# Rotary embedding in a hybrid attention layer: the sine product and its sum on GpSimd instead of VectorE, rounding and low part half a step later

## Chip, cores and metric

One core of a Trainium2 chip runs the whole layer in one launch. The metric is the device time in microseconds (us) of one execution. Below, PE is TensorE (matmuls), PEld its weight loads, DVE is VectorE, ACT is ScalarE, POOL is GpSimd and SP is SyncE, which here only issues transfers.

## The reference

A decoder layer over 2048 positions and 1024 channels. The input is normalised and modulated, multiplied by one wide input matrix, and split for two mixers: a forgetting attention of 8 heads over all earlier keys, and a banded attention (window of 128) of 8 query heads and 2 key heads with rotary positions and one sink value per head. Both are gated, joined, projected, normalised and added to the residual. Cut to what matters here:

```python
h = rms_norm(x, g_pre[l]) * (1.0 + scale[:, None, :]) + shift[:, None, :]
proj = h @ w_in[l]
qa, ka, va, fa, za, qb, kb, vb, zb = jnp.split(proj, split_points, axis=-1)
oa = forgetting_attention(qa, ka, va, fa + b_fgate[l]) * jax.nn.silu(za)
qb, kb = rope(qb, positions), rope(kb, positions)
ob = sliding_window_sink_attention(qb, kb, vb, sinks[l]) * jax.nn.silu(zb)
y = jnp.concatenate([oa, ob], axis=-1) @ w_out[l]
x = x + gate[:, None, :] * rms_norm(y, g_post[l])

def rope(x, positions):
    ...
    x1, x2 = xf[..., :half], xf[..., half:]
    return jnp.concatenate([x1 * cos - x2 * sin, x2 * cos + x1 * sin], axis=-1)
```

## The kernel before

**Precision.** Every matmul operand is kept as two f16 numbers, a rounded high part and a low part (the rest), and a product is three matmuls: high by high, high by low, low by high. So each evacuation of a result has three steps: scale it, round it to f16 on ACT, and subtract on DVE to get the low part.

**Stages.** The kernel first computes the modulation and the transposed, normalised input hT for chunk 0 of four chunks of 512 positions. Then a long list of small units (`punits`) goes over PE: slices of the input projection, eight slices of three matmuls for a tile of 128 columns by one chunk. While the first chunks are projected, the input of the next chunks is normalised on DVE (L429, with the root computed on POOL, L108 to L122), transposed on PE (L435), scaled by ACT into hT's high part and a f32 copy hf (L441), and split by DVE (L445 rounds the odd slices, L446 subtracts). Then come 32 windows of the banded attention, woven between the rest of the projection slices, from some 150 to 394 us of the span. After that runs the forgetting attention, from some 400 us, and last the output projection.

**Order.** The order on each engine is written out by hand. `after(n, f)` puts a step on a list, and `tick()` runs what is due: a step put there with n runs at the n-th tick from then. In the prologue a tick comes after every two slices (`tick2`); in the windows there are four ticks a window. Within one tick the step that was put on the list earlier runs first. Every engine works its own instructions in this order, and an instruction that waits holds all that stand behind it on that engine. An issue of a transfer by POOL (`G.dma_start`) or SP stands in that engine's queue like any other instruction.

**The rotary evacuation** (`evac_rope`, L739 to L771) runs 20 times: for the keys (kb) of the four chunks, and for the queries (qb) of four tiles by four chunks. At tick 1 ACT copies the result to qf, and SP issues four copies of 32 partitions each that swap the halves of the heads into qs (L751). At tick 2 DVE multiplies the result by the cosine into qc (L754), which frees the PSUM bank. At tick 7 DVE multiplies qs by the sine (L764) and adds it to qc (L765). At tick 8 ACT rounds qc into stg (L768), and at tick 9 DVE subtracts for the low part (L758). For keys, `finish` then has SP store stg into kst (L779); for queries stg itself is what the scores read. There is one qs and one qf; qc comes from a pool of three tiles that the gates' evacuation (tz) uses too; stg comes from a pool of two for keys and of four for queries.

**A window** (`Pair`) has: scores on PE into one PSUM tile pss (L889); masking, maxima and their scaled negative b_nb on DVE (L897 to L904); four exponentials on ACT (L911); transposes on PE (L918); folding on ACT and DVE (L927, L928); four masking selects on POOL into ptb (L932, L934); the product with the values on PE (L946); scaling on DVE (L952), and the store of its parts by POOL (L292, L285). As pss is one tile, the scores of the next window wait for the exponentials of this one. A tile's weight column is prepared ahead: load (L221, POOL), maximum (L227, DVE), its way through DRAM to all partitions (L230 mx_d and L235 mxr, both issued by POOL, the second waiting for the first to land), scale (L246 to L253, DVE), high part (L267, ACT), low part (L273, DVE).

Of the kernel before, what the change touches and what calls it, by code (L numbers as in the profile page):

```python
# [15 lines left out]
AF = mybir.ActivationFunctionType  # L16
ALU = mybir.AluOpType
# [26 lines left out]
def hybrid_layer(  # L44
# [17 lines left out]
    V, A, G, PE, SP = nc.vector, nc.scalar, nc.gpsimd, nc.tensor, nc.sync  # L62
# [88 lines left out]
    sinT = swc.tile([P, S], F32, name="sinT")  # L151
# [50 lines left out]
    def after(n, f):  # L202
        late.append([n, f])
# [535 lines left out]
    def evac_rope(ci, finish, pool):  # L739
        cols_ = slice(ci * CH, (ci + 1) * CH)  # L740

        def evac(ps, free):
            qf = swt.tile([P, CH], F32, tag="qf", name="qf")
            qs = swt.tile([P, CH], F32, tag="qs", name="qs")
            qc = op_.tile([P, CH], F32, tag="tz", name="qc")
            stg = (pool or abp).tile([P, 2, CH], F16, tag="st", name="stb")

            def copy():
                A.activation(qf[:], ps, AF.Copy, scale=PS_SCALE)
                for r in range(4):  # L750
                    SP.dma_start(qs[32 * r:32 * r + 32, :], qf[32 * (r ^ 1):32 * (r ^ 1) + 32, :])  # L751

            def cos():
                V.scalar_tensor_tensor(qc[:], ps, PS_SCALE, cosT[:, cols_], op0=ALU.mult, op1=ALU.mult)  # L754
                free()

            def low():
                V.tensor_tensor(stg[:, 1, :], qc[:], stg[:, 0, :], op=ALU.subtract)  # L758
                finish(stg)

            after(1, copy)
            after(2, cos)
            def sine():
                V.tensor_tensor(qs[:], qs[:], sinT[:, cols_], op=ALU.mult)  # L764
                V.tensor_tensor(qc[:], qc[:], qs[:], op=ALU.add)  # L765

            after(7, sine)
            after(8, lambda: A.activation(stg[:, 0, :], qc[:], AF.Copy))  # L768
            after(9, low)

        return evac  # L771

# [1011 lines left out]
```

## Time and profile before

| what | value |
|---|---|
| median of 3 runs | 1157.98 us (1157.04 to 1157.98) |
| profiled execution, its own time | 1157.8 us |
| its span, first to last instruction | 1156.1 us |
| mean granted TensorE clock | 0.996 |
| sine product L764, 20 times on DVE, shortest / median / longest | 673 / 692 / 2251 ns |
| sum L765, 20 times on DVE | 691 / 692 / 2915 ns |
| rounding L768, 20 times on ACT | 629 / 630 / 641 ns |
| low part L758, 20 times on DVE | 678 / 692 / 1732 ns |

How its rows are read. The first part of the page gives each engine's busy time, share of the span and number of instructions. A row of groups names line, engine, operation, tiles (written <- read) and shapes, the count, then busy us and mean ns of one, then the engine's idle time just before it and what ended that. A row of the timeline starts with the start and the length in us, and ends in square brackets with the idle time before it and its releaser, where there was any. A row of waits names who waited for whom, with the total, the number of times and the longest. A row of one line's instructions has shortest, median and longest ns and the first and last start. A busy PE is no proof of matmuls at full rate, since they are pipelined and their ends are modelled.

### The profile page before, as it was taken

To read this page: it belongs to the slowest core of one execution; us is meant where nothing else is said; L and a number is where in the kernel's file an instruction comes from. 1 tells how busy PE (TensorE), PEld (TensorE's weight loads), DVE (VectorE), ACT (ScalarE), POOL (GpSimd) and SP (SyncE) were. 2 spreads that over 40 slices of the span, in tenths; PEclk is the share of its full clock that TensorE was granted. 3 is DMA by queue.
4 is the path that set the end of the run, shared out by engine and by line. 5 is a ranking of instruction groups with operands and counts; after the bars stand their busy time and mean duration, and the time that the engine had idled before them with its cause. 6 is when DMAs were issued, how large, how long until landed. Compare 5 with 4: busy or idle time off the path is not lost. (4 is left out here: it accounts for less than half of the span.)

```text
span 1156.1 us, 25291 instructions
## 1 busy us (share of the span) xinstructions
PE 1116.8 (97%) x9869; PEld 656.3 (57%) x9869; DVE 930.5 (80%) x2137; ACT 661.4 (57%) x1150; POOL 207.5 (18%) x332
## 2 busy tenths in 40 slices
PE   5899999999999999999999999999999999999997
PEld 2475544577765866555555555555555555544444
DVE  7877468987888568788988899888888887878885
ACT  2876344654555421666757666666776778534332
POOL 1122134554556530010010110001000000000000
PEclk9899999999999999999999999999999999999999
DMA  9943355433243232442344342123311337686743
GB/s 333 336 116 72 87 78 96 97 63 90 52 92 88 58 87 58 73 108 29 80 64 87 84 67 70 38 49 76 45 43 34 91 101 206 140 225 197 199 135 109
DMA packets 123476, 120.10 MB, mean 104 GB/s; under 512 B 64948, under 2 KB 100828, under 8 KB 123356
## 3 DMA queue, kind: packets, MB, share of 16 engines
q1 hardware_dynamic: 112088, 85.69, 27.6%
q0 software_dynamic: 10832, 32.50, 13.5%
q8 instruction: 77, 1.26, 0.6%
q14 instruction: 43, 0.35, 0.1%
q10 hardware_dynamic: 436, 0.28, 0.1%
HBM read 64.75 MB, written 25.18 MB: 78 GB/s over the span
## 5 line engine op out<-in xcount | busy, mean ns | idle before, releaser
L1356 ACT ACTIVATE p<-sta,lift,scl_qk 128x1024 f32<-128x1024 f32 (+2 forms) x160 | 172.0, 1075 | 131.6 <-PE sta L1350 82.6
L351 PE MATMUL bk<-hT,wh_qk 128*128 128x512 f16 x768 | 194.7, 378 | 0.0
L1363 DVE TENSOR_TENSOR pha<-p,pha 128x1024 f16<-128x1024 f32 (+2 forms) x160 | 169.1, 1057 | 0.2 <-ACT pha L1360 0.2
L1303 DVE TENSOR_REDUCE a_m<-bk 128x1 f32<-128x512 f32 x192 | 130.4, 686 | 45.8 <-PE bk L1300 44.8
L1576 PE MATMUL bk<-wohl,oz 128*128 128x512 f16 x744 | 165.3, 379 | 1.1 <-DVE oz L1525 0.7
L1360 ACT ACTIVATE pha<-p 128x1024 f16<-128x1024 f32 (+2 forms) x160 | 148.1, 926 | 5.9 <-PE poa L1376 1.2
L1576 PEld LDWEIGHTS <-oz 128*128 128x128 f16 x744 | 71.9, 99 | 82.8 <-DVE oz L1525 1.8
L1376 PE MATMUL poa<-vt,pha 128*128 128x65 f16 x1088 | 116.1, 192 | 1.4 <-DVE pha L1363 1.2
L1373 PE MATMUL poa<-vt,pha 128*128 128x65 f16 x1088 | 116.6, 193 | 0.8 <-DVE ona L1382 0.7
L1375 PE MATMUL poa<-vt,pha 128*128 128x64 f16 x1088 | 116.6, 194 | 0.0
L351 PEld LDWEIGHTS <-wh_qk 128*128 128x128 f16 x768 | 72.1, 97 | 74.4 <-issue 2.1
L1349 PE MATMUL sta<-T 128*128 128x512 f16 (+1 forms) x320 | 110.9, 346 | 2.8 <-ACT p L1356 2.7
L1300 PE MATMUL bk<-T 66*128 66x512 f16 (+2 forms) x320 | 109.7, 348 | 2.4 <-DVE a_m L1303 1.9
L1373 PEld LDWEIGHTS <-pha 128*128 128x128 f16 x1088 | 101.5, 96 | 15.5 <-DVE ona L1382 1.9
L1350 PE MATMUL sta<-T 69*128 69x512 f16 (+1 forms) x320 | 109.8, 348 | 0.0
L1375 PEld LDWEIGHTS <-pha 128*128 128x128 f16 x1088 | 100.9, 97 | 11.4
L1376 PEld LDWEIGHTS <-pha 128*128 128x128 f16 x1088 | 100.8, 99 | 1.8 <-DVE pha L1363 1.7
L351 PE MATMUL bk<-hT,wh_za 128*128 128x512 f16 x384 | 99.7, 378 | 0.0
L369 PE MATMUL bk<-wh_va,hT 128*128 128x256 f16 x768 | 91.9, 273 | 0.0
L351 PE MATMUL bk<-hT,wh_zb 128*128 128x512 f16 x384 | 91.6, 379 | 0.2 <-DVE qc L754 0.2
L351 PE MATMUL bk<-hT,wh_qb 128*128 128x512 f16 x384 | 91.2, 379 | 0.0
L369 PEld LDWEIGHTS <-hT 128*128 128x128 f16 x768 | 73.3, 98 | 12.2 <-issue 2.1
(459 smaller groups left out, 1919.7 us busy)
## 6 DMA issues: line engine op xcount, KB each, us to landing
hT<-in_x_dram SPq DMA_DIRECT2D x20, 512.0 KB
wa<-in_w_ada_dram SPq DMA_DIRECT2D x16, 512.0 KB
z_d<-tz POOLq DMA_DIRECT2D x32, 256.0 KB, 3.0
T<-z_d SPq DMA_DIRECT2D x16, 512.0 KB
T<-stq SPq DMA_DIRECT2D x62, 128.0 KB
out_dram<-hT SPq DMA_DIRECT2D x15, 512.0 KB
xt<-in_x_dram SPq DMA_DIRECT2D x12, 512.0 KB
qs<-qf SPq DMA_DIRECT2D x80, 64.0 KB
```

Of the source, the lines that this page charges most:

```text
L351: PE.matmul(ps, whl[:, a, k, :], hT[ci][:, b, k, :], start=(k == 0 and n == 0), stop=(k == KT - 1 and n == 2))
L369: PE.matmul(ps[:, (u % 2) * 2 * P:(u % 2 + 1) * 2 * P], hT[ci][:, a, k, u * P:(u + 1) * P], wv[p][:, b, k, :], start=(k == 0 and n == 0), ...
L1303: V.tensor_reduce(m3[:, u, pc:pc + 1], mx[:, :w], axis=AX.X, op=ALU.max)
L1349: PE.matmul(self.st[:, o:o + w], T[:, 3, kb_], T[:, 1, qc], start=True, stop=False)
L1350: PE.matmul(self.st[:, o:o + w], T[0:XR, 2, kb_], T[0:XR, 0, qc], start=False, stop=not diag)
L1356: A.activation(self.p32[:, :self.w], self.st[:, :self.w], AF.Exp, scale=scl[f"qk{self.hd}"][:], bias=lift[:])
L1360: A.activation(self.ph[:, 0, :self.w], self.p32[:, :self.w], AF.Copy)
L1363: V.tensor_tensor(self.ph[:, 1, :self.w], self.p32[:, :self.w], self.ph[:, 0, :self.w], op=ALU.subtract)
L1373: PE.matmul(po[:, u, :], ph[:, 0, pq], vt[:, b, hd, 0:65], start=(self.first and n == 0 and u == 0), stop=False)
L1375: PE.matmul(po[:, u, 0:64], ph[:, 0, pq], vt[:, b, hd, 65:VW], start=False, stop=False)
L1376: PE.matmul(po[:, u, :], ph[:, 1, pq], vt[:, b, hd, 0:65], start=False, stop=(self.last and n == len(self.blocks) - 1))
L1576: PE.matmul(py, self.hl[:, i, k, :], w_slot(8 * j + k)[:, cc], start=(k == 0 and m_ == 0), stop=(k == KT - 1 and m_ == 2))
```

## The change

The two DVE instructions of tick 7 become two GpSimd instructions at the same tick. The rounding on ACT moves from tick 8 to tick 9 and the low part on DVE, with the keys' stores behind it, from tick 9 to tick 10. Nothing else differs.

```diff
             after(1, copy)
             after(2, cos)
             def sine():
-                V.tensor_tensor(qs[:], qs[:], sinT[:, cols_], op=ALU.mult)
-                V.tensor_tensor(qc[:], qc[:], qs[:], op=ALU.add)
+                G.tensor_tensor(qs[:], qs[:], sinT[:, cols_], op=ALU.mult)
+                G.tensor_tensor(qc[:], qc[:], qs[:], op=ALU.add)
 
             after(7, sine)
-            after(8, lambda: A.activation(stg[:, 0, :], qc[:], AF.Copy))
-            after(9, low)
+            after(9, lambda: A.activation(stg[:, 0, :], qc[:], AF.Copy))
+            after(10, low)
```

## The prediction

> **What bounds the kernel now.** I read the busy shares first, then the stretches of the span, then what TensorE (PE) waited for, then the rotary's own rows.
>
> ```profile
> span 1156.1 us, 25291 instructions
> PE 1116.8 (97%) x9869; PEld 656.3 (57%) x9869; DVE 930.5 (80%) x2137; ACT 661.4 (57%) x1150; POOL 207.5 (18%) x332
> ```
>
> PE is busy for 97% of the span; VectorE (DVE) has 20% to spare. In the stretches below (start:end and length in us, then the busy time of PE, PEld, DVE, ACT, POOL) the 20 rotary evacuations all lie in the first three.
>
> ```profile
> 45.00:110.00 65.00, 60.25 (x512) 40.77 (x512) 50.56 (x111) 45.47 (x77) 16.46 (x45) 0.97 0.48 138
> 110.00:150.00 40.00, 40.00 (x264) 22.35 (x263) 21.69 (x60) 16.86 (x27) 5.06 (x8) 1.00 0.43 83
> 150.00:400.00 250.00, 247.54 (x2350) 160.00 (x2349) 198.62 (x444) 134.18 (x432) 131.63 (x190) 1.00 0.37 81
> ```
>
> PE idles 4.75 us of the 65, nothing of the 40 and 2.46 us of the 250. So 7.2 us is the most that any relief of DVE in these stages can give; the stage behind, from 400 us, has no rotary. What PE waited for between 45 and 400 us (total, times, longest):
>
> ```profile
> PE pss L889 <- ACT sm__2471 L911: 1.9, 1, 1.9
> PE bk L351 <- DVE hT L445: 1.7, 2, 1.4
> PE bk L351 <- DVE hT L446: 1.2, 4, 0.4
> PE pss L889 <- ACT sm__2836 L911: 0.4, 1, 0.4
> ```
>
> Two places count: the split of the transposed input (hT) in the prologue, and the banded scores that need the exponentials of the window before. DVE feeds both.
>
> **What is removed.** The 20 products and 20 sums leave DVE:
>
> ```profile
> L764 DVE TENSOR_TENSOR qs<-qs,sinT 128x512 f32<-128x512 f32 x20 | 19.2, 959 | 4.1 <-DMA qs<-qf 3.7 <-issue 0.3
> L765 DVE TENSOR_TENSOR qc<-qc,qs 128x512 f32<-128x512 f32 x20 | 18.1, 904 | 0.7
> ACT stb L768 <- DVE qc L765: 36.2, 17, 3.3
> ```
>
> That is 37.3 us of DVE (19.2 + 18.1), and, since rounding comes a half step later, a chance to do other work in the 36.2 us that ScalarE (ACT) stood waiting for the sum. But PE was nearly covered through all of that, so these savings buy at most the waits above.
>
> **What is added.** GpSimd (POOL) has no row of a 128x512 f32 product. The nearest:
>
> ```profile
> L934 POOL TENSOR_SCALAR_AFFINE_SELECT ptb<-fold 128x512 f16<-128x512 f16 x62 | 46.5, 751 | 0.0
> 67.25 0.20 POOL L116 TENSOR_TENSOR rs_t<-rs_t,rs_v 128x4 f32<-128x4 f32 x1
> L547 POOL TENSOR_SCALAR_AFFINE_SELECT triu<-ones 128x128 f32<-128x128 f32 x1 | 0.3, 298 | 0.0
> 64.78 0.69 DVE L765 TENSOR_TENSOR qc<-qc,qs 128x512 f32<-128x512 f32 x1
> ```
>
> 0.20 us at 4 elements and 0.298 at 128 with one input make 0.79 ns an element. At 512 that is 0.60 us if the second input is free (low end), 1.0 us if it costs as much as the first, and 1.7 us if one colliding DVE product of 0.69 us is waited out besides (high end). I take 1.15 us, nearest to the two-input reading with a little waiting, so 2.3 us a pair in place of DVE's 1.4 us alone; 20 pairs add 46 us to POOL's 131.6 + 16.5 + 5.1 us of the three stretches, which is far from full. [...]
>
> What stands behind the pair in POOL's queue comes later by up to 2.3 us: stores, weight loads and the masking selects (L932, L934), whose results PE multiplies two windows on; the list of PE's waits has none for POOL, so this is costed at nothing, and at some 2 us a window if that cover were gone. Low (L758) and, for the keys, its four stores on SP's queue come a half step later. The tightest use of low:
>
> ```profile
> 148.49 0.69 DVE L758 TENSOR_TENSOR stb<-qc,stb 128x512 f16<-128x512 f32 x1 [0.70 <-ACT stb L768]
> L889 PE MATMUL pss<-kst,stb x384: 216/269/280, 152.7 to 394.1; 64*128 64x256 f16 x180, 64*128 64x128 f16 x12
> ```
>
> It ends at 149.2 and the first scores read it at 152.7: 3.5 us, where a half step here is two slices of a projection, six matmuls of 0.22 us or 1.3 us. So that too costs nothing.
>
> What decides is where the pair stands in POOL's queue and who waits behind the rounding on ACT's. I followed the tick lists through the source: rounding takes the place that low has now. Four places matter; at the other sixteen the pair ends before ACT gets to the rounding, or ACT is held where the next window has time left.
>
> **Place 1, keys of chunk 0: a loss.** POOL has the root of chunk 2 in front of the sine.
>
> ```profile
> 63.11 0.78 ACT L441 ACTIVATE hf<-px,Shp,Gp 128x512 f32<-128x512 f32 x1
> 65.51 0.63 ACT L768 ACTIVATE stb<-qc 128x512 f16<-128x512 f32 x1 [1.62 <-DVE qc L765]
> 66.70 1.44 ACT L441 ACTIVATE hf<-px,Shp,Gp 128x512 f32<-128x512 f32 x2
> 67.85 0.20 POOL L122 TENSOR_TENSOR rst<-rs_t,rs_y 128x4 f32<-128x4 f32 x1
> 68.08 1.42 DVE L429 TENSOR_SCALAR xt<-xt,rst 128x1024 f32<-128x1024 f32 x2 [0.96 <-POOL rst L122]
> 70.01 0.69 DVE L446 TENSOR_TENSOR hT<-hf,hT 128x512 f16<-128x512 f32 x1
> 70.62 1.41 DVE L429 TENSOR_SCALAR xt<-xt,rst 128x1024 f32<-128x1024 f32 x2
> 72.41 0.38 PE L351 MATMUL bk<-hT,wh_kb 128*128 128x512 f16 x1 [0.25 <-DVE hT L445]
> ```
>
> The sum ended at 65.5. On POOL the pair starts when the root ends: 68.05 now, some 67.2 once DVE's pair no longer lies beside the root. There the first normalisations (L429) want DVE. Taking turns: product to 68.4, normalisation (0.71) to 69.1, sum to 70.3, normalisation to 71.0. ACT, freed at 63.9, does hT and hf of slice 2 by 65.6 and then stands before the rounding until 70.3, ending it at 70.9; queued behind it are hf of slices 3 to 7, the first of which comes at 70.9 instead of 67.4. DVE does slice 2's split by 71.7, the other two normalisations by 73.1, low (moved to here) by 73.8, and only then slice 3's cast, which began at 72.0 (70.62 + 1.41). The rest of the splits follow as closely as before, and PE, which waits for this cast from 72.2 and for the next splits, waits 2 us more. Bounds: 0 if the pair runs at the low end, +3.6 if both products hold DVE for their whole length and low waits besides. I take **+2.0**.
>
> **Place 2, keys of chunk 1: a gain.**
>
> ```profile
> 86.78 0.54 POOL L235 DMA_DIRECT2D mxr<-mx_d  x1 [7.47 <-DMA mx_d<-w_mx]
> 87.32 0.69 DVE L764 TENSOR_TENSOR qs<-qs,sinT 128x512 f32<-128x512 f32 x1 [3.32 <-DMA qs<-qf]
> 88.77 0.63 ACT L768 ACTIVATE stb<-qc 128x512 f16<-128x512 f32 x1 [3.09 <-DVE qc L765]
> 97.02 0.38 PE L351 MATMUL bk<-hT,wh_kb 128*128 128x512 f16 x1 [1.43 <-DVE hT L445]
> ```
>
> DVE stood 3.3 us for the swapped rows, ACT 3.1 us for the sum. Now one hf and two squares go ahead of the rounding; the pair runs 87.3 to 89.6, or about 1.2 us later, as the stores of chunk 0's keys leave SP's queue later and the copies of chunk 1 stand behind them. ACT is 0.8 us ahead afterwards (+1.0 to -1.9 us at the ends): **-0.8**, off the 1.43 us wait.
>
> **Place 3, the fourth query chunk: a gain.**
>
> ```profile
> 190.96 2.92 DVE L765 TENSOR_TENSOR qc<-qc,qs 128x512 f32<-128x512 f32 x1
> 192.69 0.63 POOL L934 TENSOR_SCALAR_AFFINE_SELECT ptb<-fold 128x512 f16<-128x512 f16 x1
> 195.62 0.58 ACT L927 ACTIVATE fold<-pxb 128x512 f16<-128x512 f32 x1
> 199.05 0.23 DVE L904 TENSOR_SCALAR b_nb<-b_m,nscl_qb 128x4 f32<-128x4 f32 x1
> 199.32 0.46 ACT L911 ACTIVATE sm__2471<-pss,b_nb,scl_qb 128x129 f32<-128x129 f32 x1 [3.11 <-DVE b_nb L904]
> 201.24 0.83 PE L889 MATMUL pss<-kst,stb 64*128 64x256 f16 x12 [1.90 <-ACT sm__2471 L911]
> ```
>
> Without the pair (0.69 + 2.92), and low after the maxima, b_nb comes near 195.2. The pair runs on POOL behind the selects, 193.3 to 195.6, ACT rounds to 196.2, and oh and fold (0.58 each at most) let the exponentials start at 197.4 or so instead of 199.3. **-1.7** of the 1.9 (0 if POOL is slow). The like wait of 0.4 us goes too, as b_nb comes a pair earlier: **-0.4**.
>
> **Place 4, the seventh query chunk: a loss.**
>
> ```profile
> 235.61 0.55 POOL L235 DMA_DIRECT2D mxr<-mx_d  x1 [1.86 <-DMA mx_d<-w_mx]
> 235.93 0.46 ACT L911 ACTIVATE sm__3077<-pss,b_nb,scl_qb 128x129 f32<-128x129 f32 x1 [0.22 <-DVE b_nb L904]
> 239.99 0.83 PE L889 MATMUL pss<-kst,stb 64*128 64x256 f16 x12
> ```
>
> In POOL's order the pair stands behind mxr, an issue that waits for a DMA. It ends at 238.5 in this trace's time, some 1 us earlier against PE if the work before has moved up as above. Behind the rounding (0.63) queue vt's evacuation and fold (0.58 each) and four exponentials of 0.46, so these end near 242.1 or 241.1, where PE wants them at 240. **+1.1** (0 to +2.3).
>
> **Sum.** +2.0 - 0.8 - 1.7 - 0.4 + 1.1 = +0.2 us. The profiled execution took 1157.8 us (span 1156.1 and 1.7 around it), the median of the three runs is 1157.98. 1157.8 + 0.2 = **1158.0 us**: no change that a measurement tells (0.2% is 2.3 us).
>
> **Rivals.** (a) *Faster:* POOL's pair is in time everywhere but at place 1, where it costs half (+1.0): +1.0 - 1.9 - 1.9 - 0.4 = -3.2, 1154.6 us. For it speaks the 36.2 us that ACT waits no more; against it, that PE was covered for nearly all of them.
>
> [...]
>
> (c) *Slower, the queue:* POOL's blocked issues hold the pair more often than I count.
>
> ```profile
> POOL mxr L235 <- DMA mx_d<-w_mx: 84.6, 20, 9.0
> ```
>
> If place 3 gives nothing and place 4 costs 2.3: +2.0 - 0.8 - 0.4 + 2.3 = +3.1, 1160.9 us.
>
> **Numbers.** Chances: no change 0.47, (a) 0.22, (b) 0.18, (c) 0.13. So faster 0.22, same 0.47, slower 0.31. All ends together would give -4.2 and +6.9; the range 1154.2 to 1162.0, a little beyond (a) and (b) on each side, leaves out 2 in 10. The forecast's own range is 1155.7 to 1160.1.
>
> **What would show it.** Right: DVE idle or at normalisation near 64 to 68 us; rounding of chunk 0's keys ending near 71 with PE's wait for hT grown to 3 us or more; the 3.3 us DVE wait for qs gone; PE's 1.9 us wait for sm gone, and a new one near 240 us. Wrong: pairs over 2.6 us or under 1.6; new PE waits at other windows, or for the selects; a shift that arises after 400 us.

## The result, and the profile after

Run beside the kernel before on the same chip, the changed kernel took 1164.91 us (median of 4, 1163.51 to 1165.78) against 1157.98: ratio 1.0060, 95% interval 1.0042 to 1.0077. It is slower by 6.9 us; the forecast was no change, with a range that ended at 1162.0. The profiled execution took 1164.66 us.

The page's first part, and the first and third of the stretches of the span that hold the rotary (columns as before, then the granted clock, the DMA share and GB/s):

```profile
span 1162.9 us, 25283 instructions
...
PE 1121.1 (96%) x9869; PEld 658.9 (57%) x9869; DVE 913.6 (79%) x2097; ACT 662.6 (57%) x1150; POOL 253.6 (22%) x372
```

```profile
45.00:110.00 65.00, 62.04 (x513) 42.00 (x513) 51.81 (x108) 46.91 (x79) 22.46 (x50) 0.92 0.48 138
...
150.00:400.00 250.00, 242.96 (x2268) 155.91 (x2266) 177.47 (x405) 131.24 (x420) 161.73 (x216) 0.99 0.37 80
```

POOL has 46 us more, as forecast. DVE has only 17 us less, although 37.3 us were taken off it: 20 us came back as stretching of what stayed there (913.6 against 930.5 - 37.3). PE's idle time grew by 2.5 us (1162.9 - 1121.1 against 1156.1 - 1116.8), but its busy time by 4.3 us for the same 9869 matmuls. The column of the granted clock, 0.92 where it was 0.97 and 0.99 where it was 1.00, says where to look: behind place 4 the 12 matmuls of L369 are busy for 2.51 us at a granted clock of 0.55, and for 1.49 us at 1.00 in the trace of before.

What PE waited for, 45 to 440 us (total, times, longest), and ACT's row of the rounding:

```profile
PE pss L889 <- ACT sm__3076 L911: 2.9, 1, 2.9
...
PE bk L351 <- DVE hT L445: 1.7, 1, 1.7
PE pss L889 <- ACT sm__4371 L911: 1.6, 1, 1.6
PE pss L889 <- ACT sm__4982 L911: 1.0, 1, 1.0
PE pss L889 <- ACT sm__2008 L911: 0.6, 1, 0.6
PE pss L889 <- ACT sm__4219 L911: 0.5, 1, 0.5
...
ACT stb L768 <- POOL qc L765: 44.3, 13, 8.5
```

The wait for sm__2471 (place 3) is gone, a new one of 2.9 us stands near 240 us (place 4), and there are four of 0.5 us or more that the prediction did not have, all for exponentials. ACT waits for the sum fewer times (13 for 17) but longer, 44.3 us for 36.2.

PE's instructions come in the same order in both traces, so the start of each can be compared. This lag (after minus before) changes at few places:

| time in the trace of before | where | lag gained, us | forecast |
|---|---|---|---|
| 72 to 74 | place 1, the wait for hT | +1.6 | +2.0 |
| 74 to 77 | behind it, slow matmuls | +1.3 | 0 |
| 97 to 105 | place 2, keys of chunk 1 | -2.8 | -0.8 |
| 168 and 191 | exponentials of two windows | +0.9 | 0 |
| 201 to 224 | place 3 and the like wait | -2.2 | -2.1 |
| 240 | place 4, the wait | +3.0 | +1.1 |
| 241 to 243 | behind it, slow matmuls | +1.7 | 0 |
| 309 and 316 | exponentials late | +2.3 | 0 |
| 355 | 14th query chunk | +0.9 | 0 |
| 438 | a transfer | +0.4 | 0 |

The sum, with -0.2 before 72 us, is +6.9 us. (Some of the expectations below were written with slightly other readings of this lag, 1.5 for 1.7 and 2.4 for 2.3 us.) Place 4 in the timeline (start and length in us, in brackets the idle time ahead and its releaser), and then the granted clock (the third number from the end of a row) at places 1 and 4:

```profile
234.98 0.55 POOL L235 DMA_DIRECT2D mxr<-mx_d  x1 [3.62 <-DMA mx_d<-w_mx]
235.55 1.28 POOL L764 TENSOR_TENSOR qs<-qs,sinT 128x512 f32<-128x512 f32 x1
236.91 1.26 POOL L765 TENSOR_TENSOR qc<-qc,qs 128x512 f32<-128x512 f32 x1
...
238.21 0.63 ACT L768 ACTIVATE stb<-qc 128x512 f16<-128x512 f32 x1 [8.54 <-POOL qc L765]
...
239.70 0.47 ACT L911 ACTIVATE sm__3076<-pss,b_nb,scl_qb 128x129 f32<-128x129 f32 x1
...
241.63 0.83 PE L889 MATMUL pss<-kst,stb 64*128 64x256 f16 x12 [2.94 <-ACT sm__3076 L911]
242.40 2.51 PE L369 MATMUL bk<-wh_va,hT 128*128 128x256 f16 x12
```

```profile
72.01:75.42 3.41, 1.39 (x7) 0.51 (x6) 3.37 (x7) 3.41 (x6) 0.00 (x0) 1.00 0.23 53
75.42:78.84 3.42, 3.42 (x11) 1.54 (x10) 2.84 (x5) 2.85 (x4) 0.00 (x0) 0.50 0.72 167
239.26:242.68 3.42, 1.05 (x15) 0.81 (x15) 2.73 (x7) 2.32 (x10) 2.80 (x4) 1.00 0.17 41
242.68:246.09 3.41, 3.41 (x18) 2.68 (x17) 3.20 (x11) 2.24 (x5) 0.79 (x2) 0.50 0.14 42
```

POOL stands 3.6 us before mxr, whose data are not there, while the pair's data are; ACT stands 8.5 us for the pair, and four exponentials wait behind it. PE is back at 241.63 us and from 242.68 us on gets half its clock for 3.41 us: 1.7 us lost, and 1.7 us of lag. The 12 matmuls of L369 show it, 0.21 us each on average for 0.12 in the trace of before. Place 1 has the same behind its wait, half the clock from 75.42 to 78.84 us and 1.3 us of lag. Whoever looks for waits alone misses this part of the loss.

### The profile page after: what moved, and what is told of

It is laid out like the page before. It is cut to its first block, busy times and chain, and to the rows that moved or that the text cites. A ratio compares the mean times of both kernels' runs of the same rounds, so it can differ in the third digit from the quotient of the medians.

```text
span 1162.9 us, 25283 instructions
## 1 busy us (share of the span) xinstructions
PE 1121.1 (96%) x9869; PEld 658.9 (57%) x9869; DVE 913.6 (79%) x2097; ACT 662.6 (57%) x1150; POOL 253.6 (22%) x372
## 5 line engine op out<-in xcount | busy, mean ns | idle before, releaser
L369 PE MATMUL bk<-wh_va,hT 128*128 128x256 f16 x768 | 93.2, 275 | 0.0
L369 PEld LDWEIGHTS <-hT 128*128 128x128 f16 x768 | 74.0, 99 | 12.7 <-issue 2.1
```

The lines of the kernel that those rows point to most:

```text
L369: PE.matmul(ps[:, (u % 2) * 2 * P:(u % 2 + 1) * 2 * P], hT[ci][:, a, k, u * P:(u + 1) * P], wv[p][:, b, k, :], start=(k == 0 and n == 0), ...
```

## The experiments

Three theories: **late pair** (the pair ends late because of its length and of what stands ahead of it on POOL, and the work behind the rounding is late with it), **contention** (POOL's products stretch DVE's work), **delay** (the half step later costs). All kernels ran with the kernel before on the same chip; ratios are to that, with 95% intervals, and 0.001 is 1.16 us. Where nothing else is said, a diff is against the changed kernel.

### Engine and delay apart

The engine alone:

```diff
-            after(9, lambda: A.activation(stg[:, 0, :], qc[:], AF.Copy))
-            after(10, low)
+            after(8, lambda: A.activation(stg[:, 0, :], qc[:], AF.Copy))
+            after(9, low)
```

> The pair on GpSimd at tick 7, rounding at tick 8 and low part at tick 9 as before the change. Late-pair theory (the pair ends late because it takes 2.55 us and stands behind other work in POOL's queue, and ACT and all behind the rounding wait for it): the rounding meets the pair half a step earlier, ACT's waits at it grow from 44 us to 60 us or more, and the kernel is slower than the changed one, 1167 to 1180 us. Contention theory (DVE's work is stretched by POOL's products): the products are the same, so 1164 to 1166 us. Delay theory (the half step later is what costs): 1158 us, as before.

Measured: 1.0189 (1.0163 to 1.0215). Its waits of PE and ACT:

```profile
PE px L435 <- ACT hf L441: 4.3, 2, 4.0
PE pss L889 <- ACT stb L768: 3.7, 1, 3.7
...
ACT stb L768 <- POOL qc L765: 72.6, 17, 10.1
```

The delay alone:

```diff
-                G.tensor_tensor(qs[:], qs[:], sinT[:, cols_], op=ALU.mult)
-                G.tensor_tensor(qc[:], qc[:], qs[:], op=ALU.add)
+                V.tensor_tensor(qs[:], qs[:], sinT[:, cols_], op=ALU.mult)
+                V.tensor_tensor(qc[:], qc[:], qs[:], op=ALU.add)
```

> The pair stays on VectorE at tick 7, rounding at tick 9 and low part at tick 10 as in the changed kernel. Late-pair theory: ACT's 36.2 us of waiting for the sum falls below 15 us, the places with PE waits gain, nothing is added: 1154 to 1157.5 us, faster than before. Contention theory: 1157 to 1158 us. Delay theory: 1163 to 1165 us, all of the loss.

Measured: 0.9984 (0.9976 to 0.9993), faster than both kernels.

```profile
ACT stb L768 <- DVE qc L765: 12.1, 8, 3.2
```

So the change is two edits of opposite sign: the later rounding takes 24 of ACT's 36.2 us of waiting away and gains 1.9 us, and the engine alone loses 22 us. The delay theory falls. Contention, for which the rounding's tick does not matter, does not explain 1.0189 against 1.006.

### Keys and queries

The change for one kind alone (keys come with a pool, queries without):

```diff
+            E = G if pool is not None else V
+            d = 1 if pool is not None else 0
-                G.tensor_tensor(
+                E.tensor_tensor(
-            after(9, lambda: A.activation(stg[:, 0, :], qc[:], AF.Copy))
-            after(10, low)
+            after(8 + d, lambda: A.activation(stg[:, 0, :], qc[:], AF.Copy))
+            after(9 + d, low)
```

> The change for the four key chunks alone (pair on GpSimd, rounding and low part half a step later); the sixteen query chunks as before the change. In the changed kernel's trace the key chunks gain as much as they lose (PE is 2.6 us later from 72 to 76 us and 2.5 us earlier again by 105 us). Late-pair theory: 1157 to 1159 us. Contention theory: the prologue, where DVE's chain of splits is closest, carries the loss, 1161 us or more.

> The change for the sixteen query chunks alone; the key chunks as before the change. Late-pair theory: nearly all of the loss of 6.9 us arises among the windows (from 240 us on), 1163 to 1166 us, with the PE stall near 240 us again. Contention theory: under 1161 us.

Measured: keys 1.0005 (0.9996 to 1.0013), queries 1.0060 (1.0047 to 1.0074). The loss comes from the queries among the windows; the keys, in the prologue, where DVE is busy for 51.81 of 65 us in the changed kernel (177.47 of 250 us among the windows), bring none that stands clear of the noise.

### The pair's place in POOL's queue

The pair one tick earlier:

```diff
-            after(7, sine)
+            after(6, sine)
```

> The changed kernel with the pair put into the queue one tick earlier (6 instead of 7), rounding and low part at 9 and 10. Late-pair theory, the place in POOL's queue: ACT's wait at the rounding falls from 44 us to under 20, ratio 0.999 to 1.003. If the swapped rows come too late for tick 6, the pair waits for them and blocks POOL: ratio 1.003 to 1.006. Contention theory: as the changed kernel, 1.006.

The same with rounding and low part at their old ticks:

```diff
-            after(9, lambda: A.activation(stg[:, 0, :], qc[:], AF.Copy))
-            after(10, low)
+            after(8, lambda: A.activation(stg[:, 0, :], qc[:], AF.Copy))
+            after(9, low)
```

> The pair on GpSimd at tick 6, rounding and low part at their old ticks 8 and 9. Late-pair theory: what counts is the distance from the pair's place to the rounding, which is here that of the changed kernel (two ticks), but the work behind the rounding is due no later than before the change: ratio 1.003 to 1.010. If only the pair's place in POOL's queue counts: 0.999 to 1.002, as with the rounding at 9.

The pair at tick 7, rounding and low part one tick later:

```diff
-            after(9, lambda: A.activation(stg[:, 0, :], qc[:], AF.Copy))
-            after(10, low)
+            after(10, lambda: A.activation(stg[:, 0, :], qc[:], AF.Copy))
+            after(11, low)
```

> The changed kernel with rounding and low part one tick later still (10 and 11), pair at 7. Late-pair theory: ACT's wait at the rounding falls from 44 us to under 20: ratio 0.999 to 1.003, unless the low part comes too late for the scores or the keys' stores. Contention theory: 1.006, as the products are the same.

Measured: pair at 6 and rounding at 9, 1.0004 (0.9994 to 1.0014); pair at 6 and rounding at 8, 1.0067 (1.0042 to 1.0092); pair at 7 and rounding at 10, 1.0048 (1.0036 to 1.0061). The first, at place 4:

```profile
231.30 1.26 POOL L764 TENSOR_TENSOR qs<-qs,sinT 128x512 f32<-128x512 f32 x1
232.63 1.27 POOL L765 TENSOR_TENSOR qc<-qc,qs 128x512 f32<-128x512 f32 x1
...
234.43 0.55 POOL L235 DMA_DIRECT2D mxr<-mx_d  x1
...
233.94 0.63 ACT L768 ACTIVATE stb<-qc 128x512 f16<-128x512 f32 x1 [3.78 <-POOL qc L765]
```

```profile
PE 1118.3 (97%) x9869; PEld 656.5 (57%) x9869; DVE 909.4 (79%) x2097; ACT 661.5 (57%) x1150; POOL 252.2 (22%) x372
```

The pair now runs in the time that POOL spent before mxr, and mxr itself goes out no later. The loss against the kernel before is gone with all 20 pairs on POOL, which decides against contention as its cause: DVE is stretched here too, by 16 us (909.4 against 930.5 - 37.3). What is left is the distance to the delay alone, 1.0004 against 0.9984. With the rounding only two ticks behind the pair, as in the changed kernel, a loss of the same size is back, at other places (PE waits 4.0 us for hf and 3.5 us for the first queries' stb): an early place on POOL helped only where the consumer did not move up with it (1.0004 against 1.0067). The third missed its expectation: ACT's wait fell to 18.6 us, as expected, but three waits for exponentials stayed (1.3, 0.8 and 1.0 us), the clock fell to half from 358.61 to 362.02 us, and the scores waited for the low part:

```profile
PE pss L889 <- DVE stb L758: 2.4, 2, 1.5
```

### The same work on POOL, with nobody waiting for it

DVE's pair and the later rounding; behind the sum POOL does a product and a sum on the dead qs, which nothing reads:

```diff
                 V.tensor_tensor(qc[:], qc[:], qs[:], op=ALU.add)
+                G.tensor_tensor(qs[:], qs[:], sinT[:, cols_], op=ALU.mult)
+                G.tensor_tensor(qs[:], qs[:], sinT[:, cols_], op=ALU.add)
```

> VectorE does product and sum, rounding and low part are half a step later (the kernel of the delay alone, ratio 0.9984), and behind the sum GpSimd does a product and a sum of the same size on the dead qs, whose result nothing reads. [...] Late-pair theory: ratio 0.998 to 1.001. Contention theory (or the held qs, or what stands behind the pair in POOL's queue): 1.004 or more.

Measured: 1.0127 (1.0113 to 1.0141), far from what the late-pair theory said. The chain of its largest wait:

```profile
153.71 1.60 POOL L767 TENSOR_TENSOR qs<-qs,sinT 128x512 f32<-128x512 f32 x1
155.26 0.95 POOL L221 DMA_DIRECT2D wr_qb<-in_w_in_dram  x1
...
165.34 1.22 DVE L227 TENSOR_REDUCE w_mx<-wr_qb 128x1 f32<-128x1024 f32 x1 [4.73 <-DMA wr_qb<-in_w_in_dram]
...
167.92 0.63 ACT L770 ACTIVATE stb<-qc 128x512 f16<-128x512 f32 x1 [8.03 <-DVE qc L765]
...
173.69 1.47 PE L891 MATMUL pss<-kst,stb 64*128 64x256 f16 x12 [3.68 <-ACT sm__2020 L913]
```

The idle pair holds back the weight load behind it; the load lands late; DVE's maximum waits 4.7 us for it with the next real pair behind it; and so on to PE. So the theory was too narrow: what stands *behind* a pair on POOL is not free either. This wait and the slow matmuls behind it hold 6.6 of the 13.6 us that the span is longer. PE also waits 2.4 us here for the masking selects, which it does not in the changed kernel. The rest was not taken apart, so contention may have a part in it. The pair here also waits for DVE's sum (10 times, 13.9 us) and so sits later than in the changed kernel, so this size is not the changed kernel's.

### Which places

In the changed kernel some query chunks go back to DVE (counted from 0 over all 20 with the keys first, the 7th query chunk is number 10; the other kernels have `n_rope in (14, 15)`, `(10, 14, 15, 17)` and `(10, 13, 17)`):

```diff
+            n_rope = ropes[0]
+            ropes[0] += 1
             def sine():
-                G.tensor_tensor(
+                E = V if n_rope == 10 else G
+                E.tensor_tensor(
```

> The changed kernel, but for the seventh query chunk alone product and sum are on VectorE again (rounding still half a step later). It isolates the place near 240 us, where PE waits 2.9 us and then runs at a granted clock of 0.50 to 0.92 for 5 us. Late-pair theory: that wait and the slow stretch behind it both go, 4 to 5 us less than the changed kernel: ratio to before 1.002 to 1.003. Rival, the wait only moves to the next window: ratio 1.005 or more. If the slow clock does not hang on the wait: 3 us less, ratio 1.0035, and slow matmuls at 243 us all the same.

> The changed kernel with product and sum of the eleventh and twelfth query chunk on VectorE again (rounding half a step late). In the changed kernel PE loses 2.4 us between 309 and 325 us, behind these two. If they cause it (late pair, or their lying beside VectorE's short work): 1.5 to 3 us less than the changed kernel, ratio 1.0035 to 1.005. If it follows from places before (the 2.9 us wait near 240 us): 1.006 as the changed kernel.

> The changed kernel with product and sum of the 7th, 11th, 12th and 14th query chunk on VectorE again. The places behind these hold 3.0 and 1.5, 2.4, and 0.9 us of PE's lag in the changed kernel, 7.8 us in all of a net 6.9. If the sum of places holds: ratio 0.999 to 1.0015, no slower than before with 16 of 20 pairs on GpSimd. If the cost is spread over all 20 (contention, a fuller POOL): 1.0045 to 1.0055, a fifth less.

> The changed kernel with product and sum of the 7th, 10th and 14th query chunk on VectorE again. With the 7th, 11th, 12th and 14th there a PE wait of 1.4 us at 316 us was left. If the 10th chunk's pair brings it (it stands ahead of the stores, selects and weight maxima that follow on POOL's queue): that wait goes, ratio 0.9995 to 1.0010. If not: 1.001 to 1.003, the wait stays, and those of the 11th and 12th chunk come on top.

Measured: without the 7th, 1.0034 (1.0021 to 1.0048); without the 11th and 12th, 1.0044 (1.0032 to 1.0057); without the 7th, 11th, 12th and 14th, 1.0014 (1.0005 to 1.0022); without the 7th, 10th and 14th, 1.0015 (1.0006 to 1.0025). In the traces the waits near 240 and 355 us leave with the 7th and the 14th chunk: these two are shown. Without the 7th alone 4.7 us of lag went at 240 to 246 us (the clock stayed at 1.00) and 0.9 us came back later, most of it at the wait for sm__4219, now 1.3 us. With three or four chunks off POOL about three quarters of the loss are gone, so it isn't spread over the pairs. The wait at 316 us stayed in all four; in the last three, with the 10th or with the 11th and 12th chunk taken off, it was 1.4 us each time:

```profile
PE pss L895 <- ACT sm__4371 L917: 1.4, 1, 1.4
```

So neither the pairs of the 11th and 12th chunk nor that of the 10th make it. What does stays open. And the gain of the second kernel is not at its edit: up to some 290 us it is the changed kernel, yet PE's wait at 240 us was 2.1 us there, with the clock at 1.00 behind it, for 2.9 us and the fall to 0.50. One profile of a place like this is one draw.

### Half of the pair, mixed, and later

The product alone on POOL, then the pair's engine and tick by kind:

```diff
+            after(6, lambda: G.tensor_tensor(qs[:], qs[:], sinT[:, cols_], op=ALU.mult))
+            after(7, lambda: V.tensor_tensor(qc[:], qc[:], qs[:], op=ALU.add))
```

> The product on GpSimd at tick 6, the sum on VectorE at tick 7, rounding and low part at ticks 9 and 10. By the late-pair theory GpSimd's 1.27 us are over before the sum is due, VectorE is spared the product and its wait for the swapped rows: ratio 0.997 to 0.9990. By contention (products on GpSimd slow VectorE's work): 1.001 or more.

```diff
+            E, n7 = (V, 7) if pool is not None else (G, 6)
```

> The keys' product and sum on VectorE at tick 7, the queries' on GpSimd at tick 6, rounding and low part at 9 and 10 for all. With the pair on GpSimd at tick 6 throughout, PE lost 1.8 us for the keys of chunk 0 and nothing of note among the windows. Late-pair theory: that loss goes: ratio 0.9975 to 0.9995, as the delay alone. Contention theory: 1.000 or more, as 16 pairs still lie beside VectorE's work.

The third is the kernel before with the rounding at tick 10 and the low part at tick 11; the pair stays on VectorE at tick 7.

> Product and sum on VectorE at tick 7, rounding at tick 10 and low part at tick 11, one tick later than in the kernel of the delay alone (ratio 0.9984). If slack at the rounding still costs: 0.997 to 0.9985. If the scores then wait for the low part, as they did twice (2.4 us) with GpSimd's pair and these ticks: 0.9995 to 1.002.

Measured: half 1.0014 (1.0004 to 1.0024); keys on DVE and queries on POOL at tick 6, 0.9988 (0.9980 to 0.9997); pair on DVE with the rounding at 10, 0.9991 (0.9982 to 0.9999). The half kernel missed its range, and its time is one that contention allowed. Its trace points elsewhere: from 110 to 400 us its lag falls by 1.2 us, and at the keys of chunk 0 DVE's queue itself now stands for POOL, whose product is behind the root:

```profile
67.44 1.27 POOL L763 TENSOR_TENSOR qs<-qs,sinT 128x512 f32<-128x512 f32 x1
...
68.75 0.69 DVE L764 TENSOR_TENSOR qc<-qc,qs 128x512 f32<-128x512 f32 x1 [4.09 <-POOL qs L763]
```

Left on DVE for the keys and early enough for the queries, POOL's pair costs nothing, and the time is as low, within the intervals, as with the delay alone. With the rounding at tick 10 the scores wait 2.0 us for the low part, as they did with POOL's pair. None beats the delay alone.

### The low clock behind a long wait

The kernel before, its rounding of the 7th query chunk repeated (4, 6 and 10 in all), so that ACT is late with nothing of the rotary on POOL:

```diff
+                for _ in range(6 if n_rope == 10 else 1):
                     A.activation(stg[:, 0, :], qc[:], AF.Copy)
```

> The kernel before, with the rounding of the 7th query chunk done four times instead of once (the same result each time): 3 x 0.54 = 1.6 us more on ACT ahead of the exponentials that PE wants at 240 us. GpSimd computes nothing of the rotary. Theory that a late ACT is all that place 4 needs: a PE wait of 0.5 to 1.7 us near 240 us, and, as with the waits of 1.9 us and less so far, no fall of the granted clock: ratio 1.0000 to 1.0015.

> As before it, with six roundings: 5 x 0.54 = 2.7 us more on ACT. Theory that a PE wait of over some 2 us brings the granted clock down for some us behind it, whatever caused the wait: a wait of 1.6 to 2.8 us near 240 us and, if it is over 2.3 us, a granted clock of 0.5 to 0.9 from 242 to 247 us, ratio 1.002 to 1.004. Rival, the fall belongs to GpSimd's work: full clock, ratio 1.001 to 1.0025.

> As with six roundings, with ten: six gave a PE wait of 0.8 us, so four more of 0.66 us make one of some 3.4 us near 240 us, as long as in the changed kernel, with nothing of the rotary on GpSimd. Theory that the length of the wait brings the clock down: a granted clock of 0.5 to 0.9 in the 4 us behind it and 1 us or more lost there besides, ratio 1.003 to 1.005. Rival, it belongs to GpSimd's work: full clock, ratio 1.0020 to 1.003.

Measured: 0.9996 (0.9987 to 1.0005), 1.0004 (0.9995 to 1.0013), 1.0050 (1.0034 to 1.0066), with PE waits at 240 us of 0, 0.8 and 3.4 us; the first two were smaller than expected, as ACT had more time in hand there. In the trace of the longest, the wait, and the clock around it and behind it:

```profile
PE pss L898 <- ACT sm__3086 L920: 3.4, 1, 3.4
```

```profile
237.83:241.25 3.42, 1.63 (x8) 0.64 (x7) 1.19 (x3) 3.36 (x7) 0.12 (x1) 1.00 0.00 0
241.25:244.66 3.41, 1.79 (x22) 1.48 (x22) 3.22 (x12) 2.69 (x10) 3.40 (x6) 1.00 0.16 38
244.66:248.07 3.41, 3.41 (x52) 3.17 (x50) 3.34 (x8) 3.31 (x14) 1.99 (x4) 1.00 0.30 82
```

No fall of the clock. But this execution took 1160.75 us, the lowest of its four; the other three took 1162.7 to 1163.5. Whether the clock fell in those no trace shows. The theory that the length of the wait alone decides falls with this trace. For its rival, that the fall belongs to GpSimd's work, the last section has a trace that decides.

## Why the prediction was wrong

**The step that failed** is the sentence "Four places matter; at the other sixteen the pair ends before ACT gets to the rounding, or ACT is held where the next window has time left." The others held +4.1 us (0.9 at 168 and 191, 2.3 at 309 and 316, 0.9 at 355), more than any of the four. For the 0.9 at 355 us the pair is shown as the cause, by taking it away; for the wait of 1.6 us at 316 us it is not, and the places at 168, 191 and 309 us were not tried by themselves. The place at 355 us in the timeline:

```profile
354.98 0.63 POOL L934 TENSOR_SCALAR_AFFINE_SELECT ptb<-fold 128x512 f16<-128x512 f16 x1
355.58 1.26 POOL L764 TENSOR_TENSOR qs<-qs,sinT 128x512 f32<-128x512 f32 x1
356.92 1.27 POOL L765 TENSOR_TENSOR qc<-qc,qs 128x512 f32<-128x512 f32 x1
...
358.22 0.63 ACT L768 ACTIVATE stb<-qc 128x512 f16<-128x512 f32 x1 [5.00 <-POOL qc L765]
...
361.46 0.83 PE L889 MATMUL pss<-kst,stb 64*128 64x256 f16 x12 [1.03 <-ACT sm__4982 L911]
```

Here no transfer blocks POOL: four selects (the last is shown) and a pair of 2.5 us in a row are enough. The prediction looked for places with a blocked issue or a PE wait in the trace of before, and a place where ACT was just in time has neither.

**Place 4** had the right mechanism and the wrong size, +3.0 for +1.1. The step "some 1 us earlier against PE if the work before has moved up" took the lower of two values. PE had moved up by 1.4 us at 224 us, but mxr, which waits for a transfer, only by 0.6 (234.98 for 235.61): 2.1 + 0.7, and 0.2 to 0.3 for a pair of 2.6 instead of 2.3 us. Where PE runs ahead and the transfer does not, the pair behind that transfer comes later against PE, not earlier.

**The clock** was not in the sum: +1.7 us behind place 4 and +1.3 us behind place 1, which place 2 took back.

**Work behind the pair** "costed at nothing" is not shown to be wrong in the changed kernel, where PE waits for no select, but the idle copies show that the cover is thin: a pair ahead of a weight load led to a wait of 3.7 us, more than the price that the prediction named for lost cover (some 2 us a window).

**Right.** Place 1 went as written: pair behind the root, products pushed by the normalisations, rounding to 71.6. Its wait cost 1.6 us for 2.0 (PE waits 1.7 us for hT, not the 3 us or more that the prediction named as a sign), and the slow matmuls came on top. That products and normalisations take turns there was an estimate; the trace shows them longer beside one another, two normalisations 2.43 us for 1.42 and the product 1.78 us for a median of 1.28:

```profile
67.38 2.43 DVE L429 TENSOR_SCALAR xt<-xt,rst 128x1024 f32<-128x1024 f32 x2 [1.83 <-POOL rst L122]
...
67.48 1.78 POOL L764 TENSOR_TENSOR qs<-qs,sinT 128x512 f32<-128x512 f32 x1
69.34 1.60 POOL L765 TENSOR_TENSOR qc<-qc,qs 128x512 f32<-128x512 f32 x1
...
70.97 0.63 ACT L768 ACTIVATE stb<-qc 128x512 f16<-128x512 f32 x1 [5.54 <-POOL qc L765]
...
73.80 0.38 PE L351 MATMUL bk<-hT,wh_kb 128*128 128x512 f16 x1 [1.67 <-DVE hT L445]
```

Place 3 (-2.0 for -1.7) and the like wait (-0.5 for -0.4) came near their size, though 0.9 us of lag helped: the exponentials of place 3 ended 1.3 us earlier, not 1.9. Nothing but the 0.4 us of a transfer arose after 400 us. The pair's price was near, 2.6 us for 2.3:

```profile
L765 POOL TENSOR_TENSOR qc<-qc,qs 128x512 f32<-128x512 f32 x20 | 26.3, 1313 | 1.6
L764 POOL TENSOR_TENSOR qs<-qs,sinT 128x512 f32<-128x512 f32 x20 | 25.9, 1297 | 9.6 <-DMA qs<-qf 9.0 <-DVE hT L446 0.3
```

**Place 2** has the right sign by luck: -2.8 us for -0.8, and not because "ACT is 0.8 us ahead afterwards". The cast that PE waits for starts 0.07 us earlier, not 0.8 (first the row of before, then of after):

```profile
96.54 0.43 DVE L445 CAST hT<-hf 128x512 f16<-128x512 f32 x1
96.47 0.43 DVE L445 CAST hT<-hf 128x512 f16<-128x512 f32 x1
```

PE comes to it 2.7 us later, because of place 1, and so no longer meets the waits that stood there (1.43, 0.35 and smaller ones). The prediction added up two places that share one slack: what place 1 lost, place 2 gave back.

**The rivals.** (c), the queue, was the right kind with too few places. (b) has 0.18 of the chances and bounds the range above; no run shows its term. What the runs showed in its place is contention: two normalisations take 2.43 us beside the product, for 1.42 before. But 16 us of such stretching on DVE left no loss against the kernel before where the pair stood early (1.0004).

## What to carry to other kernels

A step moved to an engine that takes longer for it (here 1.28 us a product on POOL for 0.69 on DVE, medians) may need its consumer moved later and, as here, its own place moved ahead: the distance from its issue to its consumer should hold its length and the longest blocked instruction in between on its new queue (2.6 us and, before mxr, 3.6 us at place 4). Look then not only at the waits that are there, but for each use at how long ago its last input was ready; a place with no wait and no slack is where the loss appeared here, as at 355 us (0.9 us). And where a change has two parts, run each alone: here the gain lay in the part that looked like its price.

## What the runs showed of the hardware that was not expected

PE's granted clock fell to half behind waits of 2.9 us and of 1.7 and 0.35 us (places 4 and 1 of the changed kernel), 3.7 us (the idle copies) and 2.4 us (queries alone), and stayed at 1.00 behind waits of 2.1 us (without the 11th and 12th chunk) and 3.4 us (ten roundings). So the length of one wait does not decide. The 20 traces show what does, as far as they go. In each of them the stretches at half clock are 3.41 us long or twice that, but for the last one, which outlasts the kernel, and those of one trace begin at whole multiples of that length from one another: 75.42 and 242.68 us in the changed kernel are 167.26 us apart, 49 times 3.4135. Cut at these marks, the rows above show PE idle for 2.0 and 2.4 us of the stretch ahead of the two falls, while the wait of 3.4 us lay across a mark, with 1.8 us idle in one stretch and 1.6 in the next. Counted over all traces between 45 and 1150 us, half the clock followed every stretch at full clock in which PE was idle for 2.02 us or more, none with 1.79 us or less, and two of the five in between.

Whether GpSimd's work is needed, the trace without the 7th, 10th and 14th chunk decides, in a stage far behind the rotary, where POOL is busy for 0.00 us of the stretch ahead of the fall:

```profile
956.88:960.30 3.42, 1.36 (x15) 0.68 (x12) 3.28 (x10) 2.37 (x4) 0.00 (x0) 1.00 0.63 202
960.30:963.71 3.41, 3.41 (x31) 2.31 (x31) 2.69 (x4) 3.41 (x5) 0.54 (x1) 0.50 0.29 47
```

It is not. By these figures a fall costs an estimated 1.7 us (half of 3.41) beside the wait, and 1.7 and 1.3 us of lag were seen at places 4 and 1; whether one followed depended in these traces on how much of the wait lay between two marks. In this same trace the waits at place 1, as long as in the changed kernel, left the clock at 1.00 (1.78 us idle in one stretch).
